# Six of the 48 full-fp32 half blocks of a PEER layer moved in among the query blocks, and 24 instead of 21 blocks spilled

## The chip, the cores and the metric

The kernel runs on one core of a Trainium2 chip. The metric is the time of one execution on the device in microseconds (us). Five engines work side by side, each on its own queue of instructions: TensorE (PE), VectorE (DVE), ScalarE (ACT), GpSimd (POOL) and SyncE (SP, which issues most transfers).

## What is computed

A trunk of two layers on 512 tokens of width 1024, all in fp32. Each layer has a token mixer (sparse attention in the first, a state-space scan in the second) beside a cross-attention, and then a PEER block; a final norm ends it. The change lies in the PEER block alone, which runs once per layer:

```python
def peer_ffn(h, w_q, sub_keys, u, v):
    q = (h @ w_q).reshape(b, s, PEER_HEADS, 2, PEER_QDIM // 2)          # 8 heads, 2 halves of 128
    scores = jnp.einsum('bshic,ikc->bshik', q, sub_keys)                # 128 keys per half
    top_s, top_i = lax.top_k(scores, PEER_TOPK)                         # 16 of 128
    cand_s = top_s[..., 0, :, None] + top_s[..., 1, None, :]
    best_s, pos = lax.top_k(cand_s.reshape(...), PEER_TOPK)             # 16 pairs of 256
    expert = ...                                                        # key 0 * 128 + key 1
    gate = jax.nn.softmax(best_s, axis=-1)
    # per token, over its 8 * 16 chosen experts:
    act = gelu(einsum('td,thkd->thk', x, u[expert]))
    y   = einsum('thk,thkd->td', act * gate, v[expert])
```

`u` and `v` have 16384 rows of 1024 numbers each.

## The kernel before

The tokens lie in four tiles of 128 (`NT = 4`, `S = 512`, `D = 1024`, `KC = 8` slices of the width). For tile 0 the kernel gathers the chosen rows of `u` and `v`. For tiles 1 to 3 (384 tokens) it computes all experts densely, in 128 blocks of 128 experts, and multiplies by a gate matrix that is zero where an expert was not chosen. `peer` runs in three stages.

**Query stage** (lines 878 to 895). `fm_first` (L187) and `fm_block` (L178) make the 16 blocks of `q`: SP loads a block of `w_q` (tile `w_raw`, three buffers), ACT makes its rounded high part (`w_hi`, L83), POOL the remainder (`w_lo`, L84), and PE does 24 matmuls of 512 columns (`mm3`, L70 to L72: high by high, high by low, low by high, each in the fast reduced fp32 form). ACT copies the result out of PSUM (`q`, L880), PE multiplies it with the sub-keys (`sc`, L883, four full-fp32 matmuls), ACT copies the scores out (`sct`, L885), and DVE finds the 16 best of each of the four token tiles (`top16`, L1044 to L1048). After each odd block ACT casts the indices of both halves of the head (`ix`, L892: one cast for the even block, `ix0`, one for the odd, `ix1`), POOL adds the candidates (`tk_c`, L1059), and DVE finds the best pairs (`pairs`). So a pair of query blocks is one head.

**Gate stage** (L898 to L942). DVE ranks and decodes the chosen pairs (`ranks`, `decode` L1101 to L1109), PE transposes the lists (`tr`, L1119), and for each 16 tokens DVE builds four one-hot tiles (L1144 to L1147) which PE multiplies (`gate_blocks`). In between PE computes the first `SPILL = 21` of the 128 dense blocks of `u`, in full fp32 from the unsplit weights (`up`, L907): no split of the weight is needed, but a matmul takes longer. The generator `up_halves` gives half a block (4 matmuls of 384 columns) at a time, `ups(n)` does `n` halves, and after the second half of a block come a gelu (L911) and a store to DRAM (`ad`, L912).

**Expert stage** (L944 to L1037). `up_block` does a dense block of `u` in the split form, `down_block` multiplies a block's activations with the gates (L988), splits them and the block of `v`, and adds to six PSUM accumulators (`acc`, 18 matmuls of 512 columns a block). First come 8 up blocks alone, then the 21 spilled down blocks alone, whose activations are loaded back from `ad` (`act_r`, three buffers), then iterations of one up and one down block, and at the end eight down blocks. Beside them POOL gathers rows for tile 0 (`row`) and DVE uses them; `RATE` says how many per iteration: 0.4 in the spilled part, 2.5 in the main loop, 1.1 at the end, 257 steps in all.

Eight PSUM banks are given out by `use_banks`. In the query stage the transposes have two, the query blocks two (`mm`), the scores one (`sc`), and `g` names two that nothing uses there. A scheduler puts the instructions of each engine into one fixed order when the program is built; `pe_chain` (`issue_after`) keeps PE's pieces in the order in which they are written.

Of the kernel before, what the change touches and what calls it, by code (L numbers as in the profile page):

```python
# [10 lines left out]
F32 = mybir.dt.float32  # L11
# [12 lines left out]
S = 512  # L24
NT = 4
# [10 lines left out]
class Trunk:  # L36
# [792 lines left out]


    RING = 11
    SPILL = 21
    FIRST = 8

    CH = 32
# [2 lines left out]
    RATE = (0.0, 0.4, 2.5, 1.1)  # L838

    def peer(self, l, banks):  # L840
        self.use_banks(tr=banks[:2], mm=banks[2:4], sc=banks[4:5], g=banks[6:])
        nc, tc, I = self.nc, self.tc, self.I
        ND = NT - 1
        NC = ND * 128 // self.CH
        ad = self.dram.tile([self.SPILL, 128, ND * 128], F32, name=f"ad{l}")
        gd = self.dram.tile([NC, 128, 128 * self.CH], F32, name=f"gd{l}")
        with ExitStack() as es:
# [7 lines left out]
            hT = self.hT  # L855
            with ExitStack() as e2:
                pre = e2.enter_context(tc.tile_pool(name="p_pre", bufs=1))

                self.iokey = pre.tile([128, 128], F16, name="iokey")
                nc.gpsimd.iota(self.iokey, pattern=[[1, 128]], base=0, channel_multiplier=0,  # L860
                               allow_small_or_imprecise_dtypes=True)
                self.iorank = pre.tile([128, 16, 16], F16, name="iorank")
                nc.gpsimd.iota(self.iorank, pattern=[[1, 16], [0, 16]], base=0, channel_multiplier=0,
                               allow_small_or_imprecise_dtypes=True)
                sk = pre.tile([128, 2, 128], F32, name="sk")
                nc.sync.dma_start(sk, I["sub_keys"][l])
                self.norm_T(lambda t: pre.tile([128, D], F32, tag="oh", name="xs", bufs=8) if t else h0,
                            [self.x[:, t] for t in range(NT)], hT[0], hT[1], whole=hw)
                self.load_gain(3 if l == 0 else 5)
                v = pre.tile([128, NT, 16, 16], F32, name="tkv")  # L870
                iu = pre.tile([128, NT, 16, 16], U32, name="tki")
                bv = pre.tile([128, NT, 8, 16], F32, name="bv")
                bp = pre.tile([128, NT, 8, 16], U32, name="bp")

                ix = pre.tile([128, 2, NT, 8, 16, 2], F16, name="ix")
                first = self.fm_first([I["w_q"][l, b] for b in range(2)], hT)
                for b in range(16):
                    p = first[b] if b < 2 else self.fm_block(I["w_q"][l, b], hT, S)
                    q = pre.tile([128, S], F32, tag="q", name="q", bufs=2)
                    nc.scalar.copy(q, p)  # L880
                    ps = self.psum([128, NT, 128], "sc")
                    for t in range(NT):
                        nc.tensor.matmul(ps[:, t], q[:, t * 128:t * 128 + 128], sk[:, b % 2], start=True, stop=True)  # L883
                    sc = pre.tile([128, NT, 128], F32, tag="sct", name="sct", bufs=2)
                    nc.scalar.copy(sc, ps)  # L885
                    if f"sc{l}" in self.dbg:
                        nc.sync.dma_start(self.dbg[f"sc{l}"].rearrange("(t p) (b k) -> p t b k", p=128, b=16)[:, :, b], sc)
                    for t in range(NT):
                        self.top16(pre, sc[:, t], v[:, t, b], iu[:, t, b], 128)
                    if b % 2:  # L890
                        for i in range(2):
                            nc.scalar.copy(ix[:, i, :, b // 2],  # L892
                                           iu[:, :, b - 1 + i, :, None].to_broadcast([128, NT, 16, 2]))
                        self.pairs(pre, v, bv, bp, b // 2)


                self.use_banks(tr=banks[:2], up=banks[2:4], g=banks[4:])
                def up_halves():  # L898
                    for i in range(self.SPILL):
                        w = self.wst.tile([128, 1072], F32, tag="w_raw", name="w_raw", bufs=3)[:, :D]  # L900
                        w = w.rearrange("p (k c) -> p k c", k=KC)
                        nc.sync.dma_start(w, I["uT"][l, i])
                        p = self.psum([128, ND * 128], "up")
                        for k0 in range(0, KC, 4):
                            with self.pe_chain():
                                for k in range(k0, k0 + 4):
                                    mm = nc.tensor.matmul(p, w[:, k], hw[:, k], start=k == 0, stop=k == KC - 1)  # L907
                            self.pe_last = mm
                            if k0:
                                a = ring[:, KC + i % (self.RING - KC)]  # L910
                                self.gelu = nc.scalar.activation(a, p, AF.Gelu)  # L911
                                nc.sync.dma_start(ad[i], a)  # L912
                            yield
                spill = up_halves()

                def ups(n):
                    for _ in range(n):
                        next(spill)
                ups(6)
                with tc.issue_after(self.gelu.ins):  # L920
                    gates = v[:, :, :8]
                    rf = self.ranks(pre, bv, bp, gates)
                e = self.decode(pre, ix[:, :, 1], rf[:, :, 1])
                ups(5)
                sT = self.gate_lists(pre, e, gates[:, 1])
                ups(2)
                for t in range(1, NT):
                    for c in self.gate_blocks(pre, sT, gd, (t - 1) * 128 // self.CH):
                        if (c, t) != (7, NT - 1):
                            ups(1)  # L930
                        if c == 5 and t < NT - 1:
                            e = self.decode(pre, ix[:, :, t + 1], rf[:, :, t + 1])
                            ups(3)
                            sT2 = self.gate_lists(pre, e, gates[:, t + 1])
                    sT = sT2
                assert next(spill, None) is None
                e = self.decode(pre, ix[:, :, 0], rf[:, :, 0])
                nc.vector.scalar_tensor_tensor(e[0], e[0], 128.0, e[1], op0=OP.mult, op1=OP.add)
                nc.vector.tensor_copy(exi, e[0])
                nc.vector.tensor_copy(gate0, gates[:, 0].rearrange("p h s -> p (h s)"))  # L940
# [6 lines left out]
            def up_block(i):  # L947
                w = self.wblock(I["uT"][l, i], eng=nc.vector)
                p = self.psum([128, ND * 128], "mm")
                with self.pe_chain():  # L950
                    for k in range(KC):
                        self.mm3(p, (w[0][:, k], w[1][:, k]), (hT[0][:, k, 128:], hT[1][:, k, 128:]), k == 0,
                                 k == KC - 1)
                acts[i] = ring[:, i % self.RING]
                nc.scalar.activation(acts[i], p, AF.Gelu)

            def load(j):
                vr = vp.tile([128, D], F32, tag="v_raw", name="v_raw", bufs=3)
                nc.sync.dma_start(vr, I[f"v{l}"][j * 128:(j + 1) * 128, :])
                if j >= self.SPILL:  # L960
                    return vr, acts.pop(j)
                a = vp.tile([128, ND * 128], F32, tag="act_r", name="act_r", bufs=3)
                nc.sync.dma_start(a, ad[j])
                return vr, a
# [43 lines left out]
            def rows(ins, rate):  # L1008
                nonlocal done
                n = int(done + rate) - int(done)  # L1010
                done += rate
                with tc.issue_after(ins.ins):
                    for _ in range(n):
                        next(G, None)
# [3 lines left out]
            for i in range(self.FIRST):  # L1018
                up_block(self.SPILL + i)
                rows(self.last_lo, self.RATE[0])  # L1020
            loaded = {j: load(j) for j in range(3)}
            for j in range(self.SPILL):
                rows(down_block(j), self.RATE[1])
                i = self.FIRST + j // 6
                if j % 6 == 5 and i < lag:
                    up_block(self.SPILL + i)
            for i in range(self.SPILL + lag, 128 + lag):
# [265 lines left out]
```

## Time and profile before

| | |
|---|---|
| median of 3 runs | 3106.91 us (3106.91 to 3109.03) |
| the profiled execution | 3106.25 us, of it 3104.5 us span of the trace |
| PE busy | 2992.8 us, 96% of the span |
| DVE busy | 2318.5 us, 75% |
| ACT busy | 1288.2 us, 41% |
| POOL busy | 966.1 us, 31% |
| query stage of layer 0, of layer 1 | about 331 to 452 us, about 1836 to 1957 us |
| gate stage that follows, layer 0 | to about 600 us |

Busy shares are of the whole span, and stages differ: to read what an instruction costs, its stage has to be looked at. Times in the rows below count from the start of the span. Matmuls are pipelined, so that the duration of one is longer than the distance to the next; what a matmul costs on PE is read from the distance of starts.

### The profile page before, as it was taken

The page shows a single profiled execution, that of the slowest core. Times are in us where ns is not written, and L with a number is a line of the kernel's source. Part 1 is how long each engine was busy: PE and PEld are TensorE (multiplying, and loading weights), DVE is VectorE, ACT ScalarE, POOL GpSimd, SP SyncE. Part 2 cuts the span into 40 slices and gives each one's busy share as a digit, 9 for nine tenths or more (in the row PEclk, how much of TensorE's full clock was granted, in tenths as well). Part 3 has the DMA queues.
Part 4 walks back from the last instruction along what each step waited for, and adds up shares of the span by engine and source line. Part 5 has one row for each costly group of instructions (what it writes and reads, how often), then busy time and mean ns, then how long its engine had stood idle before and what let it go on. Part 6 is the DMA issues. An engine that isn't in the chain of part 4 may idle for free. (4 is left out here: it accounts for less than half of the span.)

```text
span 3104.5 us, 44164 instructions
## 1 busy us (share of the span) xinstructions
PE 2992.8 (96%) x16033; PEld 2580.1 (83%) x16038; DVE 2318.5 (75%) x4557; ACT 1288.2 (41%) x2021; POOL 966.1 (31%) x699
## 2 busy tenths in 40 slices
PE   8899999989999999999999999999999999999998
PEld 7788766778999999999878777667799999999997
DVE  5954899857777777777767669995677777777775
ACT  5574327633333333333345632583333333333332
POOL 3312320003333344444413333001233333444440
PEclk9999999999999999999999999999999999999999
DMA  4311226888888888888621122578789988889882
GB/s 161 105 45 50 75 88 250 315 280 316 304 303 310 302 316 318 306 301 310 216 91 62 55 77 69 184 296 313 268 304 316 321 299 306 310 302 317 317 280 101
DMA packets 237171, 718.63 MB, mean 231 GB/s; under 512 B 22892, under 2 KB 87960, under 8 KB 233880
## 3 DMA queue, kind: packets, MB, share of 16 engines
q1 hardware_dynamic: 157392, 438.97, 39.6%
q0 software_dynamic: 73728, 268.47, 25.2%
q10 hardware_dynamic: 5832, 8.37, 0.9%
q8 instruction: 125, 2.05, 0.3%
q14 instruction: 94, 0.77, 0.1%
HBM read 653.96 MB, written 61.75 MB: 231 GB/s over the span
## 5 line engine op out<-in xcount | busy, mean ns | idle before, releaser
L72 PE MATMUL mm<-hT,w_lo 128*128 128x384 f32 (+2 forms) x2104 | 725.3, 345 | 2.4 <-POOL w_lo L84 2.4
L70 PE MATMUL mm<-hT,w_hi 128*128 128x384 f32 (+2 forms) x2104 | 726.4, 346 | 0.5 <-ACT hT L83 0.5
L71 PE MATMUL mm<-hT,w_hi 128*128 128x384 f32 (+2 forms) x2104 | 725.4, 345 | 0.4 <-DVE hT L84 0.4
L84 DVE TENSOR_TENSOR w_lo<-w_raw,w_hi 128x1024 fp32r<-128x1024 f32 (+1 forms) x218 | 267.0, 1225 | 489.9 <-ACT w_hi L83 487.2
L71 PE MATMUL acc<-v_lo,a_hi 128*128 128x512 f32 x1536 | 604.5, 394 | 12.3 <-DVE v_lo L84 12.3
L83 ACT CAST w_hi<-w_raw 128x1024 fp32r<-128x1024 f32 (+2 forms) x311 | 321.8, 1035 | 707.5 <-PE mm L71 576.1
L1167 POOL DMA_INDIRECT row<-in_u,exi x256 | 301.2, 1177 | 1002.5 <-DVE junk L1173 676.9
L70 PE MATMUL acc<-v_hi,a_hi 128*128 128x512 f32 x1536 | 601.3, 392 | 7.4 <-ACT a_hi L83 6.1
L72 PE MATMUL acc<-v_hi,a_lo 128*128 128x512 f32 x1536 | 600.6, 391 | 0.2
L1167 POOL DMA_INDIRECT row<-in_v,exi x256 | 397.7, 1554 | 458.2 <-DVE acc L1184 377.7
L70 PEld LDWEIGHTS mm<-hT,w_hi 128*128 128x128 f32 x2104 | 396.7, 189 | 22.8 <-ACT hT L83 1.4
L71 PEld LDWEIGHTS mm<-hT,w_hi 128*128 128x128 f32 x2104 | 396.3, 188 | 21.7 <-DVE hT L84 1.3
L72 PEld LDWEIGHTS mm<-hT,w_lo 128*128 128x128 f32 x2104 | 396.0, 188 | 18.3 <-POOL w_lo L84 6.3
L71 PEld LDWEIGHTS acc<-v_lo,a_hi 128*128 128x128 f32 x1536 | 289.7, 189 | 71.9 <-DVE v_lo L84 19.2
L70 PEld LDWEIGHTS acc<-v_hi,a_hi 128*128 128x128 f32 x1536 | 289.6, 189 | 64.6 <-ACT a_hi L83 6.9
L72 PEld LDWEIGHTS acc<-v_hi,a_lo 128*128 128x128 f32 x1536 | 289.7, 189 | 63.3 <-DVE a_lo L84 1.7
L83 ACT CAST a_hi<-ring 128x384 fp32r<-128x384 f32 x214 | 110.1, 514 | 559.5 <-PE acc L71 559.5
L84 DVE TENSOR_TENSOR v_lo<-v_raw,v_hi 128x1024 fp32r<-128x1024 f32 x256 | 312.5, 1221 | 13.0 <-ACT v_hi L83 11.9
L1184 DVE SCALAR_TENSOR_TENSOR acc<-row,gact,acc 128x1024 f32<-128x1024 f32 x252 | 313.8, 1278 | 0.0
L1173 DVE SCALAR_TENSOR_TENSOR junk<-row,h 128x1024 bf16<-128x1024 f32 x256 | 311.6, 1217 | 0.1
L84 POOL TENSOR_TENSOR w_lo<-w_raw,w_hi 128x1024 fp32r<-128x1024 f32 (+3 forms) x93 | 213.8, 2305 | 285.8 <-ACT w_hi L83 266.4
L83 ACT CAST v_hi<-v_raw 128x1024 fp32r<-128x1024 f32 x256 | 268.1, 1047 | 3.7 <-DMA v_raw<-in_v 3.7
(352 smaller groups left out, 3850.3 us busy)
## 6 DMA issues: line engine op xcount, KB each, us to landing
w_raw<-in_uT SPq DMA_DIRECT2D x256, 512.0 KB, 5.1
v_raw<-in_v SPq DMA_DIRECT2D x256, 512.0 KB, 6.5
gd<-st SPq DMA_DIRECT2D x24, 2048.0 KB, 6.8
gt<-gd SPq DMA_DIRECT2D x120, 384.0 KB, 8.4
w_raw<-in_w_q SPq DMA_DIRECT2D x32, 512.0 KB, 3.2
w_raw<-in_w_o SPq DMA_DIRECT2D x16, 512.0 KB, 3.7
ad<-ring SPq DMA_DIRECT2D x42, 192.0 KB, 3.8
act_r<-ad SPq DMA_DIRECT2D x42, 192.0 KB, 3.7
```

What stands on the lines that cost most here:

```text
L70: mm(out, lhs[0], rhs[0], start=start, stop=False)
L71: mm(out, lhs[0], rhs[1], start=False, stop=False)
L72: self.pe_last = mm(out, lhs[1], rhs[0], start=False, stop=stop)
L83: self.nc.scalar.copy(hi, src)
L84: return (eng or self.nc.vector).tensor_tensor(lo, src, hi.bitcast(F32), OP.subtract)
L1167: nc.gpsimd.indirect_dma_start(out=g, out_offset=None, in_=I[name], in_offset=bass.IndirectOffsetOnAxis(ap=exi[:, s:s + 1], axis=0))
L1173: nc.vector.scalar_tensor_tensor(j, g, 1.0, h, op0=OP.mult, op1=OP.mult, accum_out=act[:, s:s + 1])
L1184: nc.vector.scalar_tensor_tensor(a, g, act[:, s:s + 1], a, op0=OP.mult, op1=OP.add)
```

## The change

`SPILL` goes from 21 to 24. The first six halves of `up_halves` (three blocks) are done in the query stage, one after each of the query blocks 4, 6, 8, 10, 12 and 14, in a PSUM bank of their own. The gate stage has the same 42 halves as before, now of the blocks 3 to 23. The main loop has three up blocks fewer per layer, and three more down blocks are in the spilled part, each with a reload of its activations. The definitions of `up_halves` and `ups` move up unchanged.

```diff
-    SPILL = 21
+    SPILL = 24
...
-        self.use_banks(tr=banks[:2], mm=banks[2:4], sc=banks[4:5], g=banks[6:])
+        self.use_banks(tr=banks[:2], mm=banks[2:4], sc=banks[4:5], up=banks[5:6])
...
                 ix = pre.tile([128, 2, NT, 8, 16, 2], F16, name="ix")
+
+                def up_halves():
+                    for i in range(self.SPILL):
+                        w = self.wst.tile([128, 1072], F32, tag="w_raw", name="w_raw", bufs=3)[:, :D]
+                        w = w.rearrange("p (k c) -> p k c", k=KC)
+                        nc.sync.dma_start(w, I["uT"][l, i])
+                        p = self.psum([128, ND * 128], "up")
+                        for k0 in range(0, KC, 4):
+                            with self.pe_chain():
+                                for k in range(k0, k0 + 4):
+                                    mm = nc.tensor.matmul(p, w[:, k], hw[:, k], start=k == 0, stop=k == KC - 1)
+                            self.pe_last = mm
+                            if k0:
+                                a = ring[:, KC + i % (self.RING - KC)]
+                                self.gelu = nc.scalar.activation(a, p, AF.Gelu)
+                                nc.sync.dma_start(ad[i], a)
+                            yield
+                spill = up_halves()
+
+                def ups(n):
+                    for _ in range(n):
+                        next(spill)
                 first = self.fm_first([I["w_q"][l, b] for b in range(2)], hT)
                 for b in range(16):
...
                         self.pairs(pre, v, bv, bp, b // 2)
-
+                    elif b >= 4:
+                        ups(1)
 
                 self.use_banks(tr=banks[:2], up=banks[2:4], g=banks[4:])
-                def up_halves():
...
                 ups(6)
```

The order in which the scheduler sets the instructions changes with it. The first place is ACT in the query stage of layer 0, from the split of the weight of query block 8 (`w_hi_4079`) on. Before it reads as follows: `q_3952` and `sct_3959` belong to block 6, `q_4016` and `sct_4023` to block 7, `w_hi_4143` to block 9; of the two casts the first is `ix1` of block 5, the second `ix0` of block 6, which needs DVE's last indices of block 6.

```order
361 L83 CAST w_hi_4079<-w_raw_4078 128x1024
362 L880 COPY q_3952<-mm_3927 128x512
363 L892 CAST ix_3401<-tki_3398 128x4x32
364 L885 COPY sct_3959<-sc_3954 128x512
365 L83 CAST w_hi_4143<-w_raw_4142 128x1024
366 L880 COPY q_4016<-mm_3991 128x512
367 L892 CAST ix_3401<-tki_3398 128x4x32
368 L885 COPY sct_4023<-sc_4018 128x512
369 L83 CAST w_hi_4236<-w_raw_4235 128x1024
```

Now the same place reads as follows. `q_3959` and `sct_3966` belong to block 6, `q_4029` and `sct_4036` to block 7, `w_hi_4163` to block 9, and `ring_3260` is the gelu of the first moved block.

```order
361 L83 CAST w_hi_4092<-w_raw_4091 128x1024
362 L902 COPY q_3959<-mm_3934 128x512
363 L914 CAST ix_3401<-tki_3398 128x4x32
364 L907 COPY sct_3966<-sc_3961 128x512
365 L890 ACT_TABLE_LOAD
366 L890 ACTIVATE ring_3260<-up_3830 128x384
367 L914 CAST ix_3401<-tki_3398 128x4x32
368 L83 CAST w_hi_4163<-w_raw_4162 128x1024
369 L902 COPY q_4029<-mm_4004 128x512
370 L907 COPY sct_4036<-sc_4031 128x512
```

Before, the copy `q` of block 7 and the split for block 9 stand ahead of `ix0` of block 6, and only `sct` of block 7 behind it. Now all three stand behind it. The same holds for the blocks 9, 11 and 13, for block 15 without a split, and for block 5 only `sct` has moved behind `ix0` (before it stood ahead). It is so in both layers.

The second place is PE at the end of the query stage of layer 0, from the last matmul of query block 15 to the transposes of the gate stage. Before (`sc_4646` is the scores of block 15):

```order
1774 L72 MATMUL mm_4619<-hT0_87,w_lo_4615 128x512
1775 L907 MATMUL up_4708<-ring_3260,w_raw_4706 128x384 x2
1776 L883 MATMUL sc_4646<-sk_3268,q_4644 128x128 x4
1777 L907 MATMUL up_4708<-ring_3260,w_raw_4706 128x384 x6
1778 L907 MATMUL up_4721<-ring_3260,w_raw_4719 128x384 x8
1779 L907 MATMUL up_4734<-ring_3260,w_raw_4732 128x384 x8
1780 L907 MATMUL up_4782<-ring_3260,w_raw_4780 128x384 x8
1781 L907 MATMUL up_4795<-ring_3260,w_raw_4793 128x384 x8
1782 L907 MATMUL up_4808<-ring_3260,w_raw_4806 128x384 x4
1783 L1119 MATMUL tr_4813<-ident_75,tk_e0_4770 128x128
1784 L1119 MATMUL tr_4813<-ident_75,tk_e1_4778 128x128
```

Now:

```order
1787 L886 MATMUL up_4747<-ring_3260,w_raw_4745 128x384 x2
1788 L905 MATMUL sc_4685<-sk_3268,q_4683 128x128 x4
1789 L886 MATMUL up_4747<-ring_3260,w_raw_4745 128x384 x6
1790 L886 MATMUL up_4760<-ring_3260,w_raw_4758 128x384 x8
1791 L886 MATMUL up_4773<-ring_3260,w_raw_4771 128x384 x8
1792 L886 MATMUL up_4821<-ring_3260,w_raw_4819 128x384 x8
1793 L886 MATMUL up_4834<-ring_3260,w_raw_4832 128x384 x8
1794 L886 MATMUL up_4847<-ring_3260,w_raw_4845 128x384 x4
1795 L1121 MATMUL tr_4852<-ident_75,tk_e0_4809 128x128
1796 L1121 MATMUL tr_4852<-ident_75,tk_e1_4817 128x128
```

Here nothing has moved: as before, 42 `up` matmuls stand between the scores of block 15 and the first transpose. The six halves of the change stand further up, in this manner (the first four rows that hold one of them and the scores `sc_3961` of block 6):

```order
1552 L886 MATMUL up_3830<-ring_3260,w_raw_3828 128x384 x3
1553 L905 MATMUL sc_3961<-sk_3268,q_3959 128x128 x4
1554 L886 MATMUL up_3830<-ring_3260,w_raw_3828 128x384
```

Three of the four matmuls of a half stand ahead of an even block's scores and one behind them (two and two at block 14), and then the matmuls of the next query block follow.

## Rows read from the trace of the kernel before

**Rows 1.** Windows: stretch, length, busy of PE, PEld, DVE, ACT, POOL, PEclk, DMA share, GB/s.
```profile
366.00:381.00 15.00, 12.84 (x57) 10.47 (x56) 14.79 (x104) 4.04 (x7) 5.94 (x4) 0.89 0.12 40
396.00:411.00 15.00, 13.47 (x66) 10.72 (x65) 13.94 (x98) 4.53 (x8) 5.87 (x4) 1.00 0.22 72
...
466.00:592.00 126.00, 124.62 (x990) 86.35 (x988) 125.77 (x125) 97.85 (x118) 0.00 (x0) 1.00 0.72 271
...
2230.00:2500.00 270.00, 270.00 (x1367) 245.94 (x1366) 201.93 (x293) 94.59 (x131) 96.73 (x83) 1.00 0.89 314
```
**Rows 2.** Waits of DVE and PE from 331 to 467 us: total, times, longest.
```profile
DVE tkv L1044 <- ACT sct L885: 11.4, 6, 7.1
...
PE sc L883 <- ACT q L880: 6.1, 5, 2.2
PE tr L1119 <- DVE tk_e L1109: 1.9, 2, 1.4
```
**Rows 3.** Timeline of ACT around block 7: start, length, instruction, idle before it.
```profile
376.22 1.05 ACT L83 CAST w_hi<-w_raw 128x1024 fp32r<-128x1024 f32 x1 [2.87 <-issue]
377.17 0.58 ACT L880 COPY q<-mm 128x512 f32<-128x512 f32 x1
381.90 0.30 ACT L892 CAST ix<-tki 128x128 f16<-128x128 uint32 x1 [4.14 <-DVE tki L1048]
382.10 0.58 ACT L885 COPY sct<-sc 128x512 f32<-128x512 f32 x1
```
**Rows 4.** Timelines of PE and DVE: scores of blocks 6 and 7, top16 of block 7.
```profile
369.68 2.07 PE L883 MATMUL sc<-sk,q 128*128 128x128 f32 x8 [2.16 <-ACT q L880]
...
377.82 1.14 PE L883 MATMUL sc<-sk,q 128*128 128x128 f32 x8
...
382.71 0.49 DVE L1044 MAX8 tkv<-sct 128x8 f32<-128x128 f32 x2 [0.85 <-ACT sct L885]
```
**Rows 5.** Timelines of PE and ACT: scores of two blocks, the first one's copy out.
```profile
340.36 1.14 PE L883 MATMUL sc<-sk,q 128*128 128x128 f32 x8
346.89 1.13 PE L883 MATMUL sc<-sk,q 128*128 128x128 f32 x8
...
341.59 0.58 ACT L885 COPY sct<-sc 128x512 f32<-128x512 f32 x1 [1.30 <-PE sc L883]
```
**Rows 6.** Timelines of ACT and PE: `ix0` of block 14, then scores 15 to transposes.
```profile
441.68 0.30 ACT L892 CAST ix<-tki 128x128 f16<-128x128 uint32 x1 [7.15 <-DVE tki L1048]
...
434.99 1.05 PE L883 MATMUL sc<-sk,q 128*128 128x128 f32 x8
435.88 27.26 PE L907 MATMUL up<-ring,w_raw 128*128 128x384 f32 x84
463.63 0.33 PE L1119 MATMUL tr<-ident,tk_e 128*128 128x128 f32 x1 [0.50 <-DVE tk_e L1109]
465.35 0.33 PE L1119 MATMUL tr<-ident,tk_e 128*128 128x128 f32 x1 [1.40 <-DVE tk_e L1109]
```
**Rows 7.** Timeline of ACT, splits of activations in layer 1: spilled part, then main loop.
```profile
2224.61 0.52 ACT L83 CAST a_hi<-act_r 128x384 fp32r<-128x384 f32 x1 [2.61 <-PE acc L71]
...
2228.69 0.52 ACT L83 CAST a_hi<-act_r 128x384 fp32r<-128x384 f32 x1 [2.61 <-PE acc L71]
...
2245.13 0.52 ACT L83 CAST a_hi<-ring 128x384 fp32r<-128x384 f32 x1 [2.62 <-PE acc L71]
...
2253.43 0.51 ACT L83 CAST a_hi<-ring 128x384 fp32r<-128x384 f32 x1 [2.61 <-PE acc L71]
```
**Rows 8.** The spilled part of layer 1: splits counted, and DVE's waits for reloads.
```profile
L83 ACT CAST a_hi<-act_r x17: 513/514/517, 2153.5 to 2228.7; 128x384 fp32r<-128x384 f32 x17
...
DVE act_r L988 <- DMA act_r<-ad: 26.0, 14, 6.2
```
**Rows 9.** Timelines of DVE and PE, end of layer 0: tile 0's last add, transposes.
```profile
1546.27 1.23 DVE L1187 TENSOR_TENSOR x<-x,acc 128x1024 f32<-128x1024 f32 x1
...
1554.22 1.94 PE L363 MATMUL tr<-ident,w_raw 128*128 128x128 f32 x8 [3.09 <-DVE w_raw L168]
...
1591.46 1.06 PE L363 MATMUL tr<-ident,w_raw 128*128 128x128 f32 x8 [0.27 <-DVE rs_ms L96]
```

More of the change, by code (lines that the diff above doesn't have):

```diff
@@ L875, in peer @@
                 ix = pre.tile([128, 2, NT, 8, 16, 2], F16, name="ix")
[L876 to L897, printed above, removed]
                 def up_halves():
@@ L918, in ups @@
                         next(spill)
+                first = self.fm_first([I["w_q"][l, b] for b in range(2)], hT)
+                for b in range(16):
+                    p = first[b] if b < 2 else self.fm_block(I["w_q"][l, b], hT, S)
+                    q = pre.tile([128, S], F32, tag="q", name="q", bufs=2)
+                    nc.scalar.copy(q, p)
+                    ps = self.psum([128, NT, 128], "sc")
+                    for t in range(NT):
+                        nc.tensor.matmul(ps[:, t], q[:, t * 128:t * 128 + 128], sk[:, b % 2], start=True, stop=True)
+                    sc = pre.tile([128, NT, 128], F32, tag="sct", name="sct", bufs=2)
+                    nc.scalar.copy(sc, ps)
+                    if f"sc{l}" in self.dbg:
+                        nc.sync.dma_start(self.dbg[f"sc{l}"].rearrange("(t p) (b k) -> p t b k", p=128, b=16)[:, :, b], sc)
+                    for t in range(NT):
+                        self.top16(pre, sc[:, t], v[:, t, b], iu[:, t, b], 128)
+                    if b % 2:
+                        for i in range(2):
+                            nc.scalar.copy(ix[:, i, :, b // 2],
+                                           iu[:, :, b - 1 + i, :, None].to_broadcast([128, NT, 16, 2]))
+                        self.pairs(pre, v, bv, bp, b // 2)
+                    elif b >= 4:
+                        ups(1)
+                self.use_banks(tr=banks[:2], up=banks[2:4], g=banks[4:])
                 ups(6)
```

## Prediction

> **What bounds the kernel now.** I first cut the span into stages, because a busy share over the whole span mixes them. In the main loop PE has no idle time at all (270.00 of 270) while DVE is three quarters busy [rows 1]: each up or down block taken out there is a saving at PE's price. In the gate stage PE and DVE are both full, 124.62 and 125.77 of 126 us [rows 1]: a late start there is not made up. In the query stage, a window of about one pair of blocks (15 us) has DVE busy for 13.94 and PE for 13.47 [rows 1]. So DVE sets the pace and PE has some 1.5 us to spare per pair. The waits then tell who releases whom: DVE waits for ACT's copy of the scores (`sct`) six times, 7.1 us of it once at the start and the rest, 4.3 us, in five waits of about 0.85; PE waits for ACT's copy `q` 6.1 us, and 1.9 us for DVE at the gate stage's first transposes [rows 2].
>
> The timeline of ACT shows how that 0.85 comes about [rows 3, 4]. The scores of block 7 start on PE at 377.82. From a start of scores to the copy `sct` it takes 1.23 us where ACT is free (340.36 to 341.59) [rows 5], so `sct` 7 could start at 379.05. It starts at 382.10, because `ix0` of block 6 stands ahead of it in ACT's queue and waits for DVE until 381.90. Then DVE begins at 382.71, 0.61 later. A ready copy does not pass a waiting cast. What stands behind `ix0` is therefore on DVE's path, and what stands ahead is not.
>
> **The change, part by part.**
>
> *The blocks saved.* Each layer loses three iterations of the main loop and gains three spilled down blocks. One iteration takes 8.30 us: so far apart lie the splits of neighbouring down blocks (2245.13 to 2253.43) [rows 7]. A spilled down block takes 4.08 (2224.61 to 2228.69) where nothing disturbs [rows 7], but over the spilled part of layer 1 17 splits lie 75.2 us apart from first to last, so 75.2 / 16 = 4.70, because DVE waits 26.0 us in all for reloads [rows 8]. I take 4.70: three more reloads come by the same road. 3 × (8.30 − 4.70) = 10.8 us per layer; 12.7 if the added ones run at 4.08, 10 if the stalls grow a little. Two layers: −21.6 (−25.4 to −20).
>
> *The six halves on PE.* 42 `up` matmuls took 27.26 us [rows 6] (the trace shows two records for each), so a half of four costs 2.60 and six cost 15.6 per layer. A query block costs 6.53 from scores to scores [rows 5], a pair 13.06, with a half 15.66. PE's waits of 6.1 and 1.9 us can swallow part. If nothing else happened, PE would come to the transposes 15.6 − 8.0 = 7.6 us later. Loads, splits, gelus and stores of the three blocks lie on SP and on ACT, which is busy 4.53 of 15 us [rows 1]; I cost them at nothing while that cover lasts. If a weight came late, PE would wait for it, and with it the next scores.
>
> *The order on ACT.* This costs more. Now `q` of an odd block, and ahead of it the split for two blocks later, stand behind `ix0`. After DVE's last index of block 6, the path used to be `ix0`, `sct` (0.20 later), DVE. Now it is `ix0`, split (0.2), `q` (0.95 later: 376.22 to 377.17), scores on PE (0.65: 377.17 to 377.82), `sct` (1.23), DVE [rows 3 to 5]: 3.03 instead of 0.20, so +2.8 us. That hits blocks 7, 9, 11 and 13. At block 5 only `sct` goes behind its `ix0`: +0.85, like the wait that the other odd blocks had [rows 4]. So DVE ends block 14 by 0.85 + 4 × 2.8 = 12.05 us later, and `ix0` of block 14 moves from 441.68 [rows 6] to 453.7. A pair then takes 15 + 2.8 = 17.8 us on DVE's path against 15.66 on PE: the longer of the two holds, and the halves run in the wait that this order makes.
>
> *The end of the query stage.* Before, the scores of block 15 stood at 434.99, well ahead of DVE, and the 42 matmuls behind them ended before DVE's list was ready (waits of 0.50 and 1.40 at `tr`) [rows 6]. Now the scores of block 15 wait for `ix0` of block 14 as well: 453.7 + 0.2 (`q`) + 0.65 = 454.6, + 0.89 to the first `up` behind them, + 27.26 = 482.7, and the second transpose at 483.1 instead of 465.35: **+17.7 us**. DVE's own delay, 12.05 + (3.03 − 0.95 − 0.20 = 1.9) = 13.9, would allow 479.3, so PE is now the late one, by 3.8 us. The gate stage has no room to make it up [rows 1]. The order is the same in both layers: +35.5 for two. Bounds: 13.9 per layer, if the gate stage swallows PE's part, and 22.4, if in addition PE's clock falls at each wait (below).
>
> *The end of layer 0.* The gathers of tile 0 have 257 steps. Before, 21 × 0.4 + 99 × 2.5 = 255.9 were done at the end of the main loop; now 24 × 0.4 + 96 × 2.5 = 249.6, and the rest goes at 1.1 per down block into the last eight. Tile 0's last add stood at 1546.27, and its transposes at 1554.22, among the last down blocks; the next tile's came at 1591.46 [rows 9]. Now tile 0's norm and transposes join the others at the end. The eight transposes took 1.94 us there [rows 9]; with a wait for the norm I take 2.5 (0, if they hide behind the other tiles, to 5). In layer 1 nothing but the final norm follows; I put it at nothing.
>
> **Sum.** 35.5 − 21.6 + 2.5 = +16.4 us on the profiled execution's 3106.25, so about 3122. The median of the runs shown is 0.66 us above the profiled one, less than 0.2% (6.2 us), which is about what a measurement of this kernel can tell from no change.
>
> **Rivals.**
>
> A. *PE fills its gaps, and DVE keeps its pace.* If the odd blocks' `q` did not in effect wait for `ix0`, only PE's work would count: 2 × 7.6 − 21.6 + 2.5 = −3.9, 3102; with the added reloads at 4.08, −7.7 and 3099. For it: PE's idle time is there [rows 1, 2]. The Trainium skill (Perfetto Trace Analysis, Matmul Optimizations) asks that all eight PSUM banks be used for more parallel work; by that rule alone this would be the outcome, since the change takes up a bank that stood idle. Against it: the copy that was held in [rows 3]. The point from which it decides: the transposes come later by 0.85 + 4d + 5.7, where d is the delay at each of the four odd blocks and 5.7 is the last block's part (441.68 to 471.0 by the steps above, less 465.35). To break even each layer may lose 10.8 − 1.25 = 9.55, so d has to be 0.75 or less instead of 2.8.
>
> B. *A weaker hold.* DVE finds slack for half of the delay, d about 1 to 1.4: 2 × (10.6 to 12.2) − 21.6 + 2.5 = +2 to +5, 3108 to 3111. For it speaks that DVE is idle 1.06 us in a pair's window [rows 1]; against it that 0.85 of this is the wait at `sct`, which the step above has already set against the new one.
>
> C. *The gate stage swallows PE's lateness.* PE would need 3.8 us there and has 1.4 [rows 1]; if it gets all of it, 2 × 13.9 − 21.6 + 2.5 = +8.7, 3115.
>
> D. *The clock falls too.* Before the scores of block 6, PE waited 2.16 us; they took 2.07 instead of 1.14, and the granted clock of that window is 0.89 [rows 1, 4]. PE's wait per pair will be 17.8 − 15.66 = 2.1, about as long. If each of five waits per layer costs the scores 0.93, that is 2 × 4.7 = +9.3: 3131. Against it: the window from 396 has 1.5 us of idle PE and a clock of 1.00 [rows 1]. The Trainium skill (TensorE: Matmul & The Clock Gate, "What's actually happening") has the array fall to 1.2 GHz when idle; by that rule these waits would give D, but the halves also make PE busier between them.
>
> **How the numbers follow.** My case has 0.39, and by the bounds above alone it lies between 3116 and 3126. A has 0.28, about half of it faster by over 0.2% (0.15) and half within (0.13). B has 0.10, within 0.2%. C has 0.13 and D 0.10, both slower. So faster 0.15, same 0.23, slower 0.62. The range from 3099 to 3131 leaves out the lowest part of A and the upper part of D.
>
> **What would show it.** Right: in the query stage of the changed kernel, PE's waits for `q` at odd blocks of about 2 us and DVE's waits for `sct` of about 3.6 us instead of 0.85; the second transpose at about 483; no wait of PE for DVE at the transposes any more; the first split of the spilled part about 17 us later, and the end of the main loop only some 7 later. Wrong: transposes at 473 or earlier (A), weights that PE waits for, or reload waits that grow by more than a quarter.

## The result and the profile after

The changed kernel takes 3127.42 us in the median (3123.91 to 3128.84, 4 runs) beside 3106.91 for the kernel before (4 runs as well): a ratio of 1.0061, 95% interval 1.0049 to 1.0073. It is slower by 0.6%, as forecast (3122, 3099 to 3131). The order on ACT, which carries the forecast, worked as worked out. Other terms were off: the end of layer 0 was charged where the net is nothing, the end of layer 1 was put at nothing and took 2.2 us, and the reload waits grew more than assumed.

The query stage first. The waits of DVE and PE from 331 to 490 us in the profile of the changed kernel, which answer to [rows 2] (total, times, longest):

```profile
DVE tkv L1046 <- ACT sct L907: 26.3, 7, 7.1
DVE oh L1146 <- ACT sT L1125: 4.3, 1, 4.3
PE sc L905 <- ACT q L902: 11.6, 6, 5.5
```

and, of the kernel before in the same stretch, the wait that answers to the second of these:

```profile
DVE oh L1144 <- ACT sT L1123: 0.9, 1, 0.9
```

DVE waited 11.4 us for `sct` before, 26.3 now. Its wait for the copies behind the transposes has grown from 0.9 to 4.3 us, and PE no longer waits for DVE at the transposes: PE is the late one there. The timeline of ACT around block 7, which answers to [rows 3], and that of PE beside it:

```profile
383.77 0.30 ACT L914 CAST ix<-tki 128x128 f16<-128x128 uint32 x1 [6.73 <-DVE tki L1050]
383.98 1.04 ACT L83 CAST w_hi<-w_raw 128x1024 fp32r<-128x1024 f32 x1
384.92 0.58 ACT L902 COPY q<-mm 128x512 f32<-128x512 f32 x1
387.72 0.58 ACT L907 COPY sct<-sc 128x512 f32<-128x512 f32 x1 [2.22 <-PE sc L905]
...
385.55 2.07 PE L905 MATMUL sc<-sk,q 128*128 128x128 f32 x8 [5.46 <-ACT q L902]
```

This is the chain of the prediction: `ix0` waits for DVE until 383.77, then come the split, `q`, the scores on PE and `sct`, at 0.21, 1.15, 1.78 and 3.95 us behind it. In [rows 3] `sct` stood 0.20 behind. PE meanwhile sat idle for 5.46 us, and its scores then took 2.07 us instead of some 1.16. The end of the stage, which answers to [rows 6]:

```profile
455.81 0.30 ACT L914 CAST ix<-tki 128x128 f16<-128x128 uint32 x1 [6.90 <-DVE tki L1050]
456.01 0.58 ACT L902 COPY q<-mm 128x512 f32<-128x512 f32 x1
...
456.64 1.16 PE L905 MATMUL sc<-sk,q 128*128 128x128 f32 x8 [1.40 <-ACT q L902]
457.64 27.26 PE L886 MATMUL up<-ring,w_raw 128*128 128x384 f32 x84
484.73 0.38 PE L1121 MATMUL tr<-ident,tk_e 128*128 128x128 f32 x2
```

`ix0` of block 14 stands at 455.81 instead of 441.68, the scores of block 15 right behind it, then the same 27.26 us of `up` matmuls, and the transposes at 484.7 with no wait ahead of them, instead of 463.63 and 465.35. How much of this is DVE's own delay can be read from the last of its lists ahead of the transposes, before and after:

```profile
465.00 0.29 DVE L1109 TENSOR_TENSOR tk_e<-tk_oh 128x128 f32<-128x128 f16 x1
...
481.02 0.29 DVE L1111 TENSOR_TENSOR tk_e<-tk_oh 128x128 f32<-128x128 f16 x1
```

That is 16.0 us later, of which 0.9 was there at the first scores of the stage (331.14 before, 332.08 after). DVE's own delay in the stage is thus 15.1 us, and PE adds 3.4 (DVE's wait of 4.3, less the 0.9 of before).

For the expert stage I read the ACT splits of activations, counted by source (count, minimum/median/maximum, first and last start), first of the kernel before, both layers:

```profile
L83 ACT CAST a_hi<-ring x107: 513/514/519, 724.6 to 1579.6; 128x384 fp32r<-128x384 f32 x107
L83 ACT CAST a_hi<-act_r x21: 506/513/517, 628.8 to 720.5; 128x384 fp32r<-128x384 f32 x21
...
L83 ACT CAST a_hi<-ring x107: 513/514/519, 2232.8 to 3082.0; 128x384 fp32r<-128x384 f32 x107
L83 ACT CAST a_hi<-act_r x21: 506/514/517, 2134.2 to 2228.7; 128x384 fp32r<-128x384 f32 x21
```

and of the changed kernel:

```profile
L83 ACT CAST a_hi<-ring x104: 513/514/519, 757.9 to 1582.3; 128x384 fp32r<-128x384 f32 x104
L83 ACT CAST a_hi<-act_r x24: 507/514/518, 647.5 to 753.8; 128x384 fp32r<-128x384 f32 x24
...
L83 ACT CAST a_hi<-ring x104: 513/514/519, 2276.4 to 3100.8; 128x384 fp32r<-128x384 f32 x104
L83 ACT CAST a_hi<-act_r x24: 508/513/517, 2161.2 to 2272.3; 128x384 fp32r<-128x384 f32 x24
```

The reader can take the whole account from these marks. Each row says when the mark comes and by how much the changed kernel's lag has grown since the mark above (lags are taken before rounding):

| mark | before | after | lag | grown by |
|---|---|---|---|---|
| first scores, layer 0 | 331.1 | 332.1 | +0.9 | +0.9, ahead of the change |
| transposes (the last that waited before), layer 0 | 465.4 | 484.7 | +19.4 | +18.4 |
| first reloaded split, layer 0 | 628.8 | 647.5 | +18.7 | −0.7 |
| first split that was not reloaded | 724.6 | 757.9 | +33.3 | +14.7, three more blocks |
| last split, layer 0 | 1579.6 | 1582.3 | +2.7 | −30.6, three fewer iterations |
| first scores of layer 1 | 1836.6 | 1844.9 | +8.3 | +5.6 |
| transposes, layer 1 | 1970.9 | 1997.6 | +26.7 | +18.4 |
| first reloaded split, layer 1 | 2134.2 | 2161.2 | +27.0 | +0.3 |
| first split that was not reloaded | 2232.8 | 2276.4 | +43.6 | +16.6, three more blocks |
| last split, layer 1 | 3082.0 | 3100.8 | +18.7 | −24.9, three fewer iterations |
| end of the span | 3104.5 | 3125.4 | +21.0 | +2.2 |

One caution for what follows. The first scores of layer 0, ahead of anything that these kernels do differently, stand anywhere from 330.9 to 334.4 us in the traces. A time of the transposes in layer 0 carries this scatter; counted from the first scores of its layer, each kernel's transposes agree between the layers to 0.4 us or better. Where the two differ, both are given.

### The profile page after: what moved, and what is told of

It is laid out like the page before. It is cut to its first block, busy times and chain, and to the rows that moved or that the text cites. A ratio compares the mean times of both kernels' runs of the same rounds, so it can differ in the third digit from the quotient of the medians.

```text
span 3125.4 us, 44070 instructions
## 1 busy us (share of the span) xinstructions
PE 3002.0 (96%) x15990; PEld 2577.4 (82%) x15990; DVE 2313.1 (74%) x4551; ACT 1283.7 (41%) x2015; POOL 967.4 (31%) x699
## 5 line engine op out<-in xcount | busy, mean ns | idle before, releaser
L70 PE MATMUL mm<-hT,w_hi 128*128 128x384 f32 (+2 forms) x2056 | 715.1, 348 | 3.3 <-ACT ring L957 2.8
L72 PE MATMUL mm<-hT,w_lo 128*128 128x384 f32 (+2 forms) x2056 | 709.7, 345 | 0.8 <-POOL w_lo L84 0.8
L71 PE MATMUL mm<-hT,w_hi 128*128 128x384 f32 (+2 forms) x2056 | 709.5, 345 | 0.4 <-DVE hT L84 0.4
L71 PE MATMUL acc<-v_lo,a_hi 128*128 128x512 f32 x1536 | 604.1, 394 | 18.7 <-DVE v_lo L84 18.7
L84 DVE TENSOR_TENSOR w_lo<-w_raw,w_hi 128x1024 fp32r<-128x1024 f32 (+1 forms) x212 | 259.7, 1225 | 474.9 <-ACT w_hi L83 474.7
L83 ACT CAST w_hi<-w_raw 128x1024 fp32r<-128x1024 f32 (+3 forms) x305 | 315.5, 1034 | 708.3 <-PE mm L71 577.1
L70 PEld LDWEIGHTS mm<-hT,w_hi 128*128 128x128 f32 x2056 | 388.4, 189 | 27.4 <-ACT ring L957 3.4
L71 PEld LDWEIGHTS mm<-hT,w_hi 128*128 128x128 f32 x2056 | 388.1, 189 | 23.6 <-DVE hT L84 1.3
L72 PEld LDWEIGHTS mm<-hT,w_lo 128*128 128x128 f32 x2056 | 387.6, 189 | 15.0 <-POOL w_lo L84 1.8
```

The source lines that it names most:

```text
L70: mm(out, lhs[0], rhs[0], start=start, stop=False)
L71: mm(out, lhs[0], rhs[1], start=False, stop=False)
L72: self.pe_last = mm(out, lhs[1], rhs[0], start=False, stop=stop)
L83: self.nc.scalar.copy(hi, src)
L84: return (eng or self.nc.vector).tensor_tensor(lo, src, hi.bitcast(F32), OP.subtract)
```

## Experiments

Two theories stood against each other. Theory 1: the lag of the query stage comes from the order on ACT. Theory 2: it comes from the halves' work on PE and from its clock, and the order on ACT is beside the point.

**e1, `q` ahead of the cast.** On all engines but ACT the order stays that of the changed kernel; on ACT only the casts move.

```diff
-                    nc.scalar.copy(q, p)
+                    held = nc.scalar.copy(q, p)
...
-                            nc.scalar.copy(ix[:, i, :, b // 2],
-                                           iu[:, :, b - 1 + i, :, None].to_broadcast([128, NT, 16, 2]))
+                            with tc.issue_after(held.ins):
+                                nc.scalar.copy(ix[:, i, :, b // 2],
+                                               iu[:, :, b - 1 + i, :, None].to_broadcast([128, NT, 16, 2]))
```

> The changed kernel, with the cast ix0 of the even block held until the copy q of the odd block is issued; on every engine but ACT the order of instructions is that of the changed kernel. Theory 1 (the ACT order is what delays DVE): DVE's waits for sct shrink from 26.3 us to about 12, PE alone now decides, the second transpose comes near 473 (465.35 + 7.6) instead of 484.9, and the kernel takes about 3127 - 2 * 11.5 = 3104 us (3099 to 3110). Theory 2 (the work of the halves on PE and the clock, not the ACT order): transposes at 480 or later and 3121 us or more.

Measured: 3108.86 us beside 3109.94 of the kernel before, ratio 0.9997 (0.9987 to 1.0006). The whole loss is gone. The waits of DVE in the same stretch, and PE's scores of block 7:

```profile
DVE tkv L1047 <- ACT sct L907: 14.2, 7, 7.1
...
384.92 1.16 PE L905 MATMUL sc<-sk,q 128*128 128x128 f32 x8 [2.55 <-ACT q L902]
...
474.89 0.38 PE L1122 MATMUL tr<-ident,tk_e 128*128 128x128 f32 x2
```

DVE's wait falls from 26.3 to 14.2 us, and the transposes come at 474.9, 9.8 us earlier. Theory 2 wanted 480 or later. Counted from the first scores, which stand at 334.35 here, the transposes come 12.1 us earlier than in the changed kernel, in both layers. With the order mended the change is worth about nothing: the transposes are still 6.3 us per layer later than before (9.5 by the time in layer 0), and that is about what three blocks save later, less 2.2 us at the end.

**e2, `sct` ahead too.** As e1, but `held` is the copy of the scores, so that nothing of an odd block stands behind `ix0`.

```diff
-                    nc.scalar.copy(sc, ps)
+                    held = nc.scalar.copy(sc, ps)
```

> The changed kernel, with both casts held until the copy sct of the odd block is issued, so that neither q nor sct of an odd block waits for ix0. Again only ACT's order differs. Theory 1: DVE loses its five waits of 0.85 us as well, but PE (15.66 us a pair against DVE's 14.1) is the bound, so nothing or little more than in the run with q alone ahead: 3100 to 3106 us. Theory 2: 3121 us or more.

Measured: 3102.13 us, ratio 0.9980 (0.9970 to 0.9991); transposes at 472.40. PE's waits for `q` from 331 us to the transposes have gone down to 1.8 us, so PE is now the bound of the stage. Counted from the first scores the transposes are 5.0 to 5.3 us later than before. Against e3 below, which has the same order on ACT and no added block, the intervals overlap: with all six halves the added blocks gain nothing that can be told.

**e3, the same on the kernel before.** The two edits of e2 on the kernel with 21 spilled blocks.

> The kernel before, with the same two casts held until sct of the odd block is issued. Theory 1: five DVE waits of 0.85 us fall away per layer and PE's waits for q shrink, DVE still bounds; the second transpose comes 4 us earlier (461), and the kernel takes 3106.9 - 8.5 = 3098.5 us (3097 to 3103). If PE's halves bound the transposes here already (they ended at 463.1 before, with PE's waits for q unchanged), only 1.9 us per layer: 3103. Theory 2: no difference over 2 us.

Measured: 3099.74 us, ratio 0.9969 (0.9953 to 0.9984). DVE's and PE's waits, and the last transpose that waits:

```profile
DVE tkv L1045 <- ACT sct L885: 7.1, 1, 7.1
PE sc L883 <- ACT q L880: 5.3, 6, 2.2
PE tr L1120 <- DVE tk_e L1110: 0.7, 1, 0.7
...
461.65 0.33 PE L1120 MATMUL tr<-ident,tk_e 128*128 128x128 f32 x1 [0.70 <-DVE tk_e L1110]
```

The five waits of 0.85 us are gone, all that is left is the 7.1 at the start, and the transposes come 3.7 us earlier (4.7 counted from the first scores, in both layers). So the wait of a ready copy behind a waiting cast had a price in the kernel before as well; the change only made it longer.

**e4, the halves moved, nothing spilled in addition.**

```diff
-    SPILL = 24
+    SPILL = 21
...
-                ups(6)
```

> The changed kernel with SPILL 21: the six halves stay among the query blocks, the six at the head of the gate stage go, and the expert stage is that of before. PE is then not late at the transposes (26 us less... 15.6 us less work ahead of them), so DVE's delay alone is seen. Theory 1: DVE's chain is as long as in the changed kernel, the second transpose near 465.35 + 14 to 16 = 479 to 481, and no iteration of the main loop is saved: 3106.9 + 2 * 15 = 3137 us (3133 to 3141). Theory 2 (PE's work): six halves moved, none added, so PE arrives no later than before at the transposes and the time is 3107 to 3112 us.

Measured: 3138.22 us, ratio 1.0089 (1.0072 to 1.0106), as theory 1 has it; the transposes come 2 us later than it had them. PE has no more work ahead of the transposes than before, yet they come at 482.9, and it is PE that waits:

```profile
DVE tkv L1045 <- ACT sct L907: 26.9, 7, 7.1
PE tr L1120 <- DVE tk_e L1110: 11.0, 1, 11.0
...
482.89 1.01 PE L1120 MATMUL tr<-ident,tk_e 128*128 128x128 f32 x2 [11.04 <-DVE tk_e L1110]
```

That is DVE's delay with PE's part taken away: counted from the first scores the second transpose comes 15.2 us later than before in layer 0 and 15.1 in layer 1, beside the 15.1 us of DVE in the changed kernel.

**e6, all 48 halves in the gate stage.** 24 blocks spilled, but the query stage left as before:

```diff
-                    elif b >= 4:
-                        ups(1)
...
-                ups(6)
+                ups(12)
```

> SPILL 24 as in the change, but all 48 halves in the gate stage, six more at its head; the query stage is that of before, with its order on ACT. The six halves, 15.6 us, then stand ahead of the transposes on a PE that was late by nothing there: second transpose near 465.35 + 13.7 = 479, with DVE waiting. Three blocks spilled instead of done in the main loop save 3 * (8.30 - 5.25) = 9.2 us per layer by the traces so far. So +4.5 per layer and +2 at the end: 3118 us (3113 to 3121). If PE had room for halves in the gate stage (rival): 3090 us or less.

Measured: 3120.97 us, ratio 1.0047 (1.0031 to 1.0064); transposes at 479.70, and DVE waits for the copies behind them:

```profile
DVE oh L1144 <- ACT sT L1123: 9.1, 1, 9.1
```

The transposes are 13.1 us per layer late by the first scores. Among the query blocks the same six halves cost 6.3 with `q` ahead (e1, 0.9997), so they are cheaper there by some 7 us per layer, but only with ACT's order mended. The changed kernel, without that, is no faster than e6 (1.0061 and 1.0047, with intervals that overlap).

**e5 and e7, why a spilled block costs more than 4.08 us.** Both are e3 with one edit:

```diff
-                a = vp.tile([128, ND * 128], F32, tag="act_r", name="act_r", bufs=3)
+                a = vp.tile([128, ND * 128], F32, tag="act_r", name="act_r", bufs=5)
```

> The kernel before with sct of the odd blocks ahead (run e3), and five instead of three buffers for the reloaded activations. Theory L (a spilled block costs more than its 4.08 us because each reload is issued only when the third buffer back is free, and lands too late): the spilled part of 21 blocks shrinks from 96 to 98 us to 86 to 90 per layer, and the kernel takes 3099.7 - 2 * 9 = 3082 us (3078 to 3088). Theory B (the transfers fill the DMA engines there, share 0.79): less than 3 us per layer, 3094 us or more.

```diff
-    RATE = (0.0, 0.4, 2.5, 1.1)
+    RATE = (0.0, 0.0, 2.6, 1.1)
```

> Run e3 with no gathered rows in the spilled part (RATE 0.0 instead of 0.4 there, 2.6 instead of 2.5 in the main loop). Theory B (DMA engines shared with the gathers make the reloads late): the spilled part shrinks by 4 us or more per layer, 3092 us or less. Theory L (buffers): by less than 2 us per layer, 3097 us or more.

Measured: e5 3095.67 us, ratio 0.9961 (0.9948 to 0.9973); e7 3094.12, 0.9956 (0.9939 to 0.9973). Theory L failed. DVE's waits for reloads from 622 to 722 us, in e3 and then with five buffers:

```profile
DVE act_r L989 <- DMA act_r<-ad: 28.7, 16, 5.2
...
DVE act_r L989 <- DMA act_r<-ad: 29.0, 13, 6.1
```

The buffers took none of the waiting away; there are fewer waits, and they are longer. (The edit also moves some instructions of DVE in this part.) The part from the first accumulating matmul to the first split that is not reloaded takes 95.1 us in layer 0 and 95.7 in layer 1, where e3 has 97.5 and 95.4. PE's waits there (e5):

```profile
PE acc L71 <- DVE v_lo L84: 8.7, 7, 2.6
```

Before the edit PE waited 6.0 us for `v_lo` and 3.4 for `a_hi` in that stretch. In e7 DVE's waits for reloads there are 23.0 us and the part takes 93.9 and 95.8 us, not 4 us less either; its time lies between what theory B (3092 or less) and theory L (3097 or more) had. Both kernels are some 4 to 6 us below e3, 2 to 4 when each is set against the kernel before in its own session, with intervals that overlap e3's. What holds the blocks back is settled by neither.

**e8, e9, and e11, e12: how many halves are free.** The mended order with two halves (after the query blocks 6 and 10) and 22 spilled blocks, and with four (4, 6, 10, 12) and 23:

```diff
-    SPILL = 24
+    SPILL = 23
...
-                    elif b >= 4:
+                    elif b in (4, 6, 10, 12):
                         ups(1)
```

> The change at a third of its size with sct of the odd blocks ahead: SPILL 22, one half each after the query blocks 6 and 10. Two halves are 5.2 us of PE, and PE waits 5.3 us for q there in run e3. If PE's gaps take them (theory 1: the idea pays as long as the halves fit), the second transpose stays near 461.7 to 463 and one spilled block saves 3.05 us per layer: 3099.7 - 5 = 3095 us (3092 to 3098). If they do not fit (the gaps are too short for a half, and PE is the bound at the transposes): second transpose near 466, 3099.7 + 4 = 3104 us.

> Between runs e2 (24, six halves) and e8 (22, two halves): SPILL 23, one half each after the query blocks 4, 6, 10 and 12, with sct of the odd blocks ahead. Four halves are 10.4 us of PE where about 5 us were waits. By theory 1 (the halves are free only up to PE's waits) the second transpose comes about 5 us later than in e8, near 467, one more spilled block saves 3 us per layer, and the time lies between the two: 3097 us (3094 to 3101). If a rule of the kind 'more blocks moved, more saved' held, it would be 3090 us or less.

e8 took 3092.41 us, ratio 0.9952 (0.9933 to 0.9971), with its transposes at 461.8: two halves are free. e9, e10 and the repeats of e8 (e11) and e3 (e12) ran on one chip.

> Run e8 once more, beside e9 and e12 on one chip, so that 21, 22 and 23 spilled blocks are compared directly: 5 to 8 us below e12.

> Run e3 once more, beside e9 and e11 on one chip: 7 to 10 us below the kernel before.

| kernel | spilled | time | ratio to before (95%) | transposes, layer 0 | second transpose after the first scores, layers 0 and 1 |
|---|---|---|---|---|---|
| e12 | 21 | 3100.90 | 0.9970 (0.9957 to 0.9982) | 462.4 | 129.5, 129.5 |
| e11 | 22 | 3093.78 | 0.9957 (0.9943 to 0.9971) | 463.0 | 129.9, 129.9 |
| e9 | 23 | 3080.41 | 0.9913 (0.9899 to 0.9926) | 465.1 | 132.6, 132.5 |
| e2, in another session | 24 | 3102.13 | 0.9980 (0.9970 to 0.9991) | 472.4 | 139.3, 139.6 |

My expectation of e9 (3097) was wrong, and by more than the size of anything it reckoned with; the time falls where it put the rule that it argued against (more blocks moved, more saved: 3090 or less), which e2 with 24 contradicts. What it said of the query stage held roughly: counted from the first scores the transposes come 2.7 us later than with 22 (5 expected) and 6.7 to 7.1 earlier than with 24, so the price of a half climbs once PE's waits have run out. With 22 there are 2.5 us of waits for `q` left (e8), with 23 0.3; with 24 PE is the bound. The rest did not go by one block more or less. The counts of splits of e9:

```profile
L83 ACT CAST a_hi<-ring x105: 513/514/519, 733.0 to 1567.6; 128x384 fp32r<-128x384 f32 x105
L83 ACT CAST a_hi<-act_r x23: 507/513/516, 628.5 to 729.0; 128x384 fp32r<-128x384 f32 x23
...
L83 ACT CAST a_hi<-ring x105: 513/514/519, 2223.0 to 3055.6; 128x384 fp32r<-128x384 f32 x105
L83 ACT CAST a_hi<-act_r x23: 507/516/516, 2119.5 to 2218.9; 128x384 fp32r<-128x384 f32 x23
```

The spilled part, from the first accumulating matmul to the first split that is not reloaded, takes 103.9 and 102.0 us with 23 blocks, 101.7 and 101.4 with 22 (e11), and 110.7 and 110.5 with 24 (e2). That reads as if the 23rd block cost 1 to 2 us and the 24th 7 to 8, but it is one profile each, and this part scatters: with 21 blocks it took 95.1 to 100.0 us (the kernel before, e3, e4, e12), with 22 in e8 99.4 and 105.6, with 24 109.1 to 113.6 (the changed kernel, e1, e2, e6). The means of 21 and of 24 blocks, 96.9 and 111.3, are 4.8 us per block apart.

The other part is clear of that scatter. From the last split of layer 0 to the first scores of layer 1 there are 256.7 us with 23, 256.2 with 22, 261.2 with 24. This is explained by the place of tile 0's last add and transposes. In e9 they stand among the last down blocks:

```profile
1557.40 1.22 DVE L1190 TENSOR_TENSOR x<-x,acc 128x1024 f32<-128x1024 f32 x1
...
1563.99 1.06 PE L363 MATMUL tr<-ident,w_raw 128*128 128x128 f32 x8 [0.77 <-DVE w_raw L168]
```

and in the changed kernel behind them:

```profile
1582.08 1.22 DVE L1189 TENSOR_TENSOR x<-x,acc 128x1024 f32<-128x1024 f32 x1
...
1589.61 1.06 PE L363 MATMUL tr<-ident,w_raw 128*128 128x128 f32 x8 [0.27 <-DVE w_raw L168]
```

With 23 blocks, 23 × 0.4 + 97 × 2.5 = 251.7 of the 257 steps are done ahead of the tail, with 24 blocks 249.6. The place has a price on both sides: the main loop of layer 0 takes 5.8 us longer than that of layer 1 in the kernel before (855.0 against 849.3), 1.9 with 22 and 23 blocks, and 0.0 with 24. So 22 and 23 blocks are the cheap place for tile 0's end, and 21 and 24 are not. Whether the 24th block of the spilled part costs more than the 23rd is not shown.

**e10, both reload edits on e8.**

> Run e8 with five reload buffers and no gathers in the spilled part. Runs e5 and e7 gave 4 and 6 us on the kernel of run e3, each within the scatter of the runs. If these gains are real and add, 3084 us (3080 to 3088); if they are scatter or attack the same wait, 3088 to 3094.

Measured: 3083.74 us, ratio 0.9915 (0.9902 to 0.9929), 10 us below e11 on the same chip. The gains of e5 and e7 are thus real together; of the 5.1 us between the two profiled spans 4.3 lie in the spilled parts (99.6 and 99.2 us), though DVE still waits 30.9 us for reloads in layer 0. Four halves, 23 blocks and these two edits were not run together. The best that were run are e9 and e10, 0.9% below the kernel before.

## Why the prediction was right, and where it was not

The terms of the sum, both layers together, beside what the marks give:

| term | forecast | measured |
|---|---|---|
| ahead of the first scores of layer 0 | not in it | +0.9 |
| query stage, to the transposes | +35.5 | +36.8 |
| gate stage | 0 | −0.4 |
| three spilled blocks for three iterations (a saving of 24.9 per layer for the iterations, as in layer 1) | −21.6 | −18.5 |
| end of layer 0 (the other 5.7 of its main loop, and what follows) | +2.5 | −0.2 |
| end of layer 1 | 0 | +2.2 |
| sum | +16.4 | +21.0 |

*The order on ACT: right, in mechanism and nearly in size.* The step gave 17.7 us per layer at the transposes; it was 18.4 in each. Its pieces stand in the rows above: the split, `q` and scores behind `ix0` take 0.21, 0.94 and 0.63 us, as summed. DVE's waits for `sct` of blocks 9, 11 and 13 are 3.7 us, where 3.6 was given as the sign. The slow scores of block 7 (2.07 us, 0.9 more than the others) are as much as the excess. e1 and e4 show the cause from both sides: move the copies ahead and the loss goes; leave them and take PE's extra work away and DVE is as late.

*PE late at the transposes: right.* 3.8 us were worked out, and PE adds 3.4 to DVE's 15.1 (13.9 worked out). Rival C, that the gate stage swallows it, failed: the lag shrinks by 0.7 us there in layer 0 and grows by 0.3 in layer 1.

*The clock, rival D: once, not five times.* The wait of 5.46 us ahead of block 7's scores is followed by slow ones, as that of 2.16 us in [rows 4] was; the windows of that stretch in the changed kernel have a mean granted clock of 0.77 (part of it at 1.2 GHz, the rest at 2.4), then 1.00 (all at 2.4 GHz):

```profile
381.00:396.00 15.00, 10.45 (x40) 8.48 (x41) 10.20 (x71) 4.04 (x7) 5.28 (x4) 0.77 0.16 57
396.00:411.00 15.00, 14.67 (x65) 11.28 (x64) 11.20 (x77) 4.51 (x8) 4.05 (x4) 1.00 0.21 72
```

The later waits are shorter (2.02 ahead of block 13's scores), and these scores take 1.16 us. It is the same in both layers. The Trainium skill (TensorE: Matmul & The Clock Gate, "What's actually happening") has an idle array fall to half its clock; the trace agrees for this wait, with scores of 2.07 us, and shows nothing of it for the others. The length of the wait alone does not tell: scores of layer 1 in the kernel before, and of layer 0 in e4:

```profile
1875.18 1.16 PE L883 MATMUL sc<-sk,q 128*128 128x128 f32 x8 [2.13 <-ACT q L880]
...
423.94 1.67 PE L905 MATMUL sc<-sk,q 128*128 128x128 f32 x8 [2.02 <-ACT q L902]
```

*A spilled block: a sign of being wrong came, and the price held only within the scatter.* The prediction took 4.70 us from the blocks that were there, and named reload waits that grow by more than a quarter as a sign against it. They did. DVE's waits for reloads over the spilled part, layer 0 before and after, then layer 1 before and after:

```profile
DVE act_r L988 <- DMA act_r<-ad: 26.4, 15, 5.1
DVE act_r L990 <- DMA act_r<-ad: 36.0, 16, 4.5
...
DVE act_r L988 <- DMA act_r<-ad: 28.8, 15, 6.2
DVE act_r L990 <- DMA act_r<-ad: 39.8, 18, 5.7
```

That is over a third more for three blocks on 21. The iterations saved gave 24.9 us per layer, as reckoned, and the three blocks added cost 14.7 and 16.6: 4.9 and 5.5 each. This made the sum 3 us too small, but with 95.1 to 100.0 us for the same 21 blocks in different profiles, 3 us in two layers are not clear of the scatter, and the 4.8 us of the means above is the term's own price.

*The end of layer 0: a charge without its credit.* The step charged 2.5 us for tile 0's norm and transposes at the end. What follows the last split does take 5.6 us more, but these transposes had cost PE 5.7 in the last down blocks before (30.6 − 24.9 on the way to the last split), which the step forgot, though the wait of 3.09 us stood in [rows 9]: the net is nothing. The prediction's sign, the end of the main loop some 7 us later, was 2.7 for this reason.

*The end of layer 1: put at nothing, 2.2 us.* The same move happens there. Tile 0's last add, before and after:

```profile
3054.84 1.22 DVE L1187 TENSOR_TENSOR x<-x,acc 128x1024 f32<-128x1024 f32 x1
...
3100.57 1.22 DVE L1189 TENSOR_TENSOR x<-x,acc 128x1024 f32<-128x1024 f32 x1
```

From the last split to the end there are 24.7 us in each of the four kernels with 24 blocks and 22.5 in all the others.

*Rival A: its mechanism is real, and is not what this kernel does.* PE's gaps do take halves: two for 0.4 us (e8), four for 3. With all six and `q` ahead (e1) the transposes come 6.3 us late per layer, less than A's 7.6. The result is that of the kernel before (0.9997) where A had 3102, because the three blocks saved some 18 us in the two layers of e1 instead of 21.6, and because of the 2.2 us at the end. The Trainium skill (Perfetto Trace Analysis, Matmul Optimizations) asks for all PSUM banks to be used. Here the bank that stood idle, filled with six halves, brought a loss of 0.6%; with the order on ACT mended two and four halves paid (e8, e9), and six paid nothing that can be told beyond the mended order (e2 against e3).

## What to carry to other kernels

When work is put into the gaps of one engine, read the order of the engine that serves both: on ACT's queue an instruction that waited held every ready one behind it, and a scheduler may put a ready copy behind a cast that waits for somebody else, as it did here. Look for the same thing in the kernel as it is, where it may already cost something (e3: 0.3% for two lines). Count the gaps before filling them, and then run a little less and a little more as well: neither the gaps nor the sum pointed to four halves. When a piece of work that other work waits for may fall on either side of a stage's end, look for its place in the trace before charging it, on both sides. And repeat the kernel before reading a few microseconds from one profile.

## What the runs showed that was not expected

The time against the number of spilled blocks is no straight line: 3100.9, 3093.8, 3080.4 and 3102.1 us for 21, 22, 23 and 24. From 23 to 24 the profiled span grows by some 19 us (3078.1 to 3097.3): 15.5 up to the ends of the two gate stages, 15.3 in the two spilled parts, 4.5 between the layers and 2.2 at the end, less the 18.4 of the main loops. The last three come back in every kernel with 24 blocks; the split of the first two rests on one profile of e9. And more buffers for the reloads (e5) took away none of DVE's waits for them (28.7 us before, 29.0 after): so three buffers alone were not what held them back, plain as it looked.
